# x in 4 KB runs with its norm weights, first tiles split by engine, squares on GpSimd, a new tile order

## The chip, the cores and the metric

The kernel runs on one core of one Trainium2 chip. The metric is the device time of one execution in microseconds; less is better. Inside the core, five engines run programs of their own and meet at semaphores: PE (TensorE, matrix products), ACT (ScalarE), DVE (VectorE), POOL (GpSimd) and SP, which here only issues the transfers.

## The reference, cut to what matters

One decoder layer over 512 tokens and 1024 channels. The part that the change touches is the beginning: the norm of x and the wide projection of it.

```python
u = rms_norm(h, g_pre)            # h = x, [512, 1024]
cols = u @ w_in                   # 1024 -> 6272 columns
# A: block-sparse attention on q, k, v, gate columns (512 each)
# B: RWKV-7 recurrence on r, k, v, gate (512 each) and two low-rank inputs (64 + 64)
merged = sigmoid(gate_a) * (yA @ p_a) + sigmoid(gate_b) * (yB @ p_b)
h = h + rms_norm(merged @ w_out, g_post)
h = h + sigmoid(h @ w_ple_gate) * (p @ w_ple_up)
```

## The kernel before, in words

Everything lies transposed: 128 channels on the partitions, 512 tokens along the row, eight channel groups kt = 0 to 7. A product in full precision is done as three products of a cheaper kind: every operand is split into a high part (the value rounded to the matmul's format) and a low part (the rest), and `mm3` runs high by high, high by low and low by high. ACT makes the high parts by a copy, DVE the low parts by a subtraction.

w_in is cut into tiles of 128 columns, named by what they give: k, r, v, z (RWKV), Q, K, V, Z (attention), g (merge gates), four or sixteen of each. A tile takes 24 matmuls of 512 columns (8 channel groups by 3 products). Four tiles come first (`first_tiles`, line 649): k0, r0, v0 and the low-rank tile, and these multiply x itself, high and low (`xh`, `xl`, made by `x_split`, line 615, times the norm weight g_pre), since the norm's factor for each token can be applied to their results. Their weights are split in quarters by `first_split`. The tiles k0 and r0 are run in two halves of 256 tokens (their results are called `s` in the rows), so that they can begin when half of x is there; then v0 (`y`) and the low-rank tile (`c`). Ahead of them stand `WARM` = 12 matmuls on zeros that keep TensorE busy while the first data comes.

In the meantime `squares` and `pre_norm` (lines 707 and 714) square x, add the eight channel groups (three additions on DVE, over 1024, 512 and 256 elements of a row), sum over the partitions by a product with ones (`g<-ones,rms`), take the inverse root in a string of short DVE instructions, spread it by a product with the identity (`g<-cst,rb`), and make the normed u: eight products `uf` on DVE, eight copies `u_hi` on ACT, eight subtractions `u_lo` on DVE.

From there the other 44 tiles (`FILL`, line 44; `fill`, line 819; results `pp`) run on u. They are the filling: whenever the recurrence or the attention has no product ready, PE takes the next matmul of a fill tile. After them come the merge, the output projection and the last gate, in the order `LAST`.

The order on each engine is fixed when the program is built: the kernel is written as streams (generators), and `Plan` picks again and again the stream that can start first by assumed durations, with ranks (`RC`, `RR_`, `RI` and others) and bonuses between streams that are close. An engine then runs its list strictly in order. `Queue` (line 310) assumes when a transfer has landed. All transfers are issued by SP, in program order: half of x in two pieces, the vectors (`vec`, g_pre among them), the first weights.

Of the kernel before, what the change touches and what calls it, by code (L numbers as in the profile page):

```python
# [26 lines left out]
F32 = mybir.dt.float32  # L27
# [8 lines left out]
T = 512  # L36
# [7 lines left out]
FILL = """  # L44
K0 g0 r1 Z0 v1 V0 g1 Q0 g2 k1 r2 g3 k2 z0 Q1 Z1 v2 K1 V1 z1 r3 k3 g4
v3 g5 V2 Z2 g6 K2 g7 g8 Q2 g9 g10 g11 V3 Z3 K3 Q3 z2 g12 g13 z3 g14 g15
"""
# [5 lines left out]
GROUPS = (0, 1), (2,), (3,)  # L53
WARM = 12
LARGE = 0.01796
BW = 0
SAME = 0.03
URGENT = 5
RC, RR_, RI, RP, RA, RE, RW = 10, 7, 6, 4, 5, 4, 3
WR, WA, WC = 0.0, 0.0, 0.0  # L60

VEC = {}
_o = 0
for _n, _k in (("g_pre", 8), ("g_post", 8), ("mu", 17), ("a0", 4), ("k_k", 4), ("k_a", 4), ("r_k", 4),
               ("ln_w", 4), ("ln_b", 4), ("w0", 4)):
    VEC[_n] = _o
    _o += _k
# [243 lines left out]
class Queue:  # L311


    def __init__(self, real, plan):
        self.real, self.plan = real, plan
        self.issue = self.move = 0.0

    def dma_start(self, out, src):
        self.real.dma_start(out, src)
        spot = lambda a: (a.tensor.name, a.offset)  # L320
        self.issue = max(self.issue, self.plan.cur.now, self.plan.written.get(spot(src), ("Q", 0.0))[1]) + 0.5
        self.move = max(self.move, self.issue + 1.6) + math.prod(out.shape) / 92000
        self.plan.written[spot(out)] = "Q", self.move
        return self.move


@with_exitstack
def hybrid_kernel(ctx: ExitStack, tc, xT, pT, wu, wda, wmain, wpab, wout, wpg, vec_in, cst_in, oneh, relb, wupa,
# [208 lines left out]
    st = start_stack.enter_context(tc.tile_pool(name="start", bufs=1))  # L537
    x_sb = st.tile([128, 8, T], F32, name="x_sb")
    xh = st.tile([128, 8, T], F32R, name="xh")
# [12 lines left out]
    def load_x(h, q):  # L552
        ks = slice(4 * q, 4 * q + 4)
        plan.marks[f"dx{h}{q}"] = sp.dma_start(x_sb[:, ks, HALF[h]], xT[:, ks, HALF[h]])

    def load_first(src):
        raw, plan.marks[f"dw{len(sraw)}"] = load_raw(src, st if len(sraw) > 1 else None)
        sraw.append(raw)

    load_x(0, 0)  # L560
    there = sp.dma_start(vec, vec_in)
    load_first(wmain[0])
    load_x(0, 1)
# [51 lines left out]
    def x_split(h, kt):  # L615
        c = HALF[h]
        yield ("wait", f"dx{h}{kt // 4}")
        if kt % 2:
            yield "A"
            act.activation(xh[:, kt, c], x_sb[:, kt, c], AF.Copy, scale=V("g_pre", kt))  # L620
        else:
            yield "D"
            dve.tensor_scalar(xh[:, kt, c], x_sb[:, kt, c], V("g_pre", kt), None, op0=OP.mult)
        yield "D"
        dve.scalar_tensor_tensor(xl[:, kt, c], x_sb[:, kt, c], V("g_pre", kt), xh[:, kt, c].bitcast(F32),
                                 op0=OP.mult, op1=OP.subtract)
        plan.mark(f"x{h}{kt}")
# [79 lines left out]
    def squares(h, sq):  # L707
        for kt in range(8):
            yield ("wait", f"dx{h}{kt // 4}")
            yield "A"  # L710
            act.activation(sq[:, kt, :], x_sb[:, kt, HALF[h]], AF.Square)
            plan.mark(f"sq{h}{kt}")

    def pre_norm():
        pb, fb = yield from take()
        sqs = [st.tile([128, 8, 256], F32, tag="sq", name="sq", bufs=2) for _ in range(2)]
        for h, sq in enumerate(sqs):
            plan.spawn(squares(h, sq), 0.1)
        for h, sq in enumerate(sqs):
            for kt in range(8):  # L720
                yield ("wait", f"sq{h}{kt}")
            for w in (4, 2):
                yield "D"
                dve.tensor_tensor(sq[:, 0:w], sq[:, 0:w], sq[:, w:2 * w], op=OP.add)
            yield "D"
            dve.tensor_tensor(rms[:, HALF[h]], sq[:, 0], sq[:, 1], op=OP.add)
        yield "P"
        for tt in range(4):
            pe.matmul(pb[:, tt:tt + 1], rms[:, tt * 128:tt * 128 + 128], ones, start=True, stop=True)
        ms, rs, tn = (st.tile([128, 4], F32, name=n) for n in ("ms4", "rs4", "tn4"))  # L730
        yield "D"
        dve.tensor_scalar(ms, pb[:, 0:4], 1.0 / 1024, RMS_EPS, op0=OP.mult, op1=OP.add)
        plan.mark(fb)
        yield from rsqrt(rs, ms, tn)
        rb = at.tile([128, T], F32, tag="bt0", name="rb4").rearrange("p (a b) -> p a b", b=128)
        yield "D"
        dve.tensor_scalar(rb, rs.unsqueeze(2).to_broadcast([128, 4, 128]), RS, None, op0=OP.mult)
        pr, fr = yield from take()
        yield "P"
        for tt in range(4):  # L740
            pe.matmul(pr[:, tt * 128:tt * 128 + 128], rb[:, tt, :], ident, start=True, stop=True)
        for kt in range(8):
            yield "D"
            tag = ("kb", "rb", "rb", "vb", "vb", "zt", "zt", "est")[kt]
            uf = (at if kt > 4 else krv).tile([128, T], F32, tag=tag, name="uf", bufs=BUFS[tag])
            dve.scalar_tensor_tensor(uf, x_sb[:, kt, :], V("g_pre", kt), pr, op0=OP.mult, op1=OP.mult)
            plan.spawn(norm_split(kt, uf), 0.5)
        yield "A"
        act.activation(rms, pr, AF.Copy)
        plan.mark(fr)  # L750
        plan.mark("rms")

    def norm_split(kt, uf):
        yield "A"
        act.activation(u_hi[:, kt, :], uf, AF.Copy)
        yield "D"
        dve.tensor_tensor(u_lo[:, kt, :], uf, u_hi[:, kt, :].bitcast(F32), op=OP.subtract)
        plan.mark(f"u{kt}")
# [60 lines left out]
    def fill(kinds):  # L819
        for i, (w, j) in enumerate(kinds):  # L820
            if w in "krv" and j >= BUFS[w + "b"]:
                yield ("wait", f"used{w}{j - BUFS[w + 'b']}")
            if w == "z":
# [187 lines left out]
    def rwkv(j):  # L1011
# [88 lines left out]
        dve.tensor_tensor(k2, k, fk, op=OP.mult)  # L1100
        plan.mark(f"usedk{j}")
        yield "D"
# [41 lines left out]
        yield ("wait", f"sv{j}")  # L1144
        plan.mark(f"usedv{j}")

        for g in range(4):
            if g:
                yield ("wait", f"gram{j}.{g - 1}")
            if g == 2:  # L1150
                yield ("wait", f"w1{j}.4")
                plan.mark(f"usedr{j}")
            gA, fA = yield from take()
# [282 lines left out]
    def late_tiles():  # L1436
# [25 lines left out]
        for q in range(2):  # L1462
            yield ("wait", f"o{2 + q}")
            sp.dma_start(F["x"][:, 4 * q:4 * q + 4, :], xT[:, 4 * q:4 * q + 4, :])

# [147 lines left out]
def arrange(inputs):  # L1613
# [7 lines left out]
    a = {  # L1621
        "xT": tiles(g["x"][0].T),
        "pT": tiles(g["p"][0, 0].T),
# [29 lines left out]
```

## Time and profile before

| | |
|---|---|
| median of 3 runs | 575.1 us (573.61 to 575.67) |
| the profiled execution | 574.87 us, of which 573.1 us are the span |
| PE busy | 558.6 us (97%) |
| DVE busy | 419.7 us (73%) |
| ACT busy | 298.7 us (52%) |
| POOL busy | 3.9 us (1%) |
| mean DMA rate | 116 GB/s |
| mean granted TensorE clock | 0.994 of full |

The span is what the profiler saw from the first to the last instruction; the time is 1.77 us longer. The share of busy time is an average over a short beginning, in which PE waits, and a long rest, in which it hardly does.

### The profile page before, as it was taken

To read this page: it belongs to the slowest core of one execution; us is meant where nothing else is said; L and a number is where in the kernel's file an instruction comes from. 1 tells how busy PE (TensorE), PEld (TensorE's weight loads), DVE (VectorE), ACT (ScalarE), POOL (GpSimd) and SP (SyncE) were. 2 spreads that over 40 slices of the span, in tenths; PEclk is the share of its full clock that TensorE was granted. 3 is DMA by queue.
4 is the path that set the end of the run, shared out by engine and by line. 5 is a ranking of instruction groups with operands and counts; after the bars stand their busy time and mean duration, and the time that the engine had idled before them with its cause. 6 is when DMAs were issued, how large, how long until landed. Compare 5 with 4: busy or idle time off the path is not lost.

```text
span 573.1 us, 10476 instructions
## 1 busy us (share of the span) xinstructions
PE 558.6 (97%) x4080; PEld 454.0 (79%) x4080; DVE 419.7 (73%) x973; ACT 298.7 (52%) x610; POOL 3.9 (1%) x17
## 2 busy tenths in 40 slices
PE   5899999999999999999999999999999999999997
PEld 3886878777777787777777877788788898999886
DVE  5997678879878887789986775659756666478623
ACT  6638563665357576546664565566433245543311
POOL 0000100000000000000000000000000000000000
PEclk8899999999999999999999999999999999999999
DMA  8321523124321112422322213325356458502211
GB/s 297 134 73 65 207 98 112 55 75 143 108 79 68 56 62 66 159 94 74 111 93 87 82 56 111 125 79 187 125 202 219 168 188 325 202 10 66 93 38 55
DMA packets 27417, 66.61 MB, mean 116 GB/s; under 512 B 2879, under 2 KB 7487, under 8 KB 27112
## 3 DMA queue, kind: packets, MB, share of 16 engines
q1 hardware_dynamic: 27368, 65.95, 33.0%
q8 instruction: 32, 0.52, 0.4%
q14 instruction: 17, 0.14, 0.1%
HBM read 56.74 MB, written 11.82 MB: 120 GB/s over the span
## 4 chain that ended last, share of the span: by engine, by line
PE 88%; DVE 7%; DMA 2%; ACT 1%; issue 1%; SPq 0%; DVEq 0%; ACTq 0%
PE pp L295 50%; PE s L295 13%; PE g L295 12%; PE c L295 8%; PE y L295 5%; DMA x_sb<-xT 1%; DVE Ep L295 1%; DVE wlo L295 1%; DVE xl L295 1%; DMA yf<-yB_dram 1%; DVE X L295 0%; DVE h_lo L295 0%; ACT En L295 0%; DVE Y L295 0%; DVE xh L295 0%
## 5 line engine op out<-in xcount | busy, mean ns | idle before, releaser
L295 PE MATMUL pp<-u_hi,whi 128*128 128x512 f32 x360 | 145.7, 405 | 0.4 <-DVE kl L295 0.4
L295 PE MATMUL pp<-u_lo,whi 128*128 128x512 f32 x360 | 145.3, 403 | 0.0
L295 PE MATMUL pp<-u_hi,wlo 128*128 128x512 f32 x360 | 144.6, 402 | 0.0
L295 ACT ACTIVATE whi<-raw 128x1024 fp32r<-128x1024 f32 (+1 forms) x86 | 71.5, 847 | 78.8 <-PE pp L295 51.2
L295 DVE TENSOR_TENSOR wlo<-raw,whi 128x1024 fp32r<-128x1024 f32 (+1 forms) x86 | 81.6, 960 | 32.7 <-ACT whi L295 32.2
L295 PEld LDWEIGHTS pp<-u_hi,whi 128*128 128x128 f32 x360 | 67.7, 188 | 14.8 <-PE pp L295 0.8
L295 PEld LDWEIGHTS pp<-u_hi,wlo 128*128 128x128 f32 x360 | 67.7, 188 | 13.2 <-issue 0.7
L295 PEld LDWEIGHTS pp<-u_lo,whi 128*128 128x128 f32 x360 | 67.8, 188 | 12.2 <-issue 0.6
L295 ACT ACTIVATE P<-P,sml 128x128 f32<-128x128 f32 (+3 forms) x32 | 17.8, 557 | 15.8 <-DVE sml L295 14.6
L295 DVE SCALAR_TENSOR_TENSOR SV<-c,D,sd 64x64 f32<-64x64 f32 x56 | 15.9, 283 | 5.9 <-PE c L295 4.8
L295 ACT ACTIVATE sd<-SV,D 64x64 f32<-64x64 f32 x56 | 19.3, 344 | 1.0
L295 DVE TENSOR_TENSOR W<-g,cst 64x128 f32<-64x128 f32 (+1 forms) x64 | 17.2, 290 | 0.7
L295 DVE CUSTOM_DVE_ANT_0 P<-s,bt 128x128 f32<-128x128 f32 (+3 forms) x32 | 14.7, 485 | 3.9 <-PE s L295 3.8
L295 PEld LDWEIGHTS c<-SV,W 128*64 128x64 f32 x240 | 9.5, 136 | 9.5 <-issue 5.9
L295 PE MATMUL pp<-m_hi,whi 128*128 128x512 f32 (+1 forms) x48 | 17.0, 354 | 0.0
L295 PE MATMUL pp<-m_lo,whi 128*128 128x512 f32 (+1 forms) x48 | 17.0, 354 | 0.0
L295 PE MATMUL pp<-m_hi,wlo 128*128 128x512 f32 (+1 forms) x48 | 17.0, 354 | 0.0
L295 ACT ACTIVATE Xt<-y 128x512 f16<-128x512 f32 x20 | 11.9, 594 | 9.7 <-PE y L295 9.6
L295 DVE TENSOR_TENSOR Z<-c,lvl 128x512 f16<-128x512 f32 x20 | 13.7, 687 | 3.3 <-PE c L295 3.2
L295 ACT ACTIVATE W<-g 128x128 f32<-128x128 f32 x32 | 7.1, 274 | 15.8 <-PE g L295 15.8
L295 PE MATMUL g<-W,BK 64*128 64x128 f32 x128 | 15.0, 310 | 0.0
L295 DVE SCALAR_TENSOR_TENSOR t<-gb,pp 128x512 f32<-128x512 f32 (+1 forms) x8 | 5.2, 655 | 12.5 <-PE pp L295 12.5
(362 smaller groups left out, 1251.1 us busy)
## 6 DMA issues: line engine op xcount, KB each, us to landing
raw<-wmain SPq DMA_DIRECT2D x48, 512.0 KB, 3.3
g_dram<-gst SPq DMA_DIRECT2D x16, 256.0 KB, 2.0
raw<-wpab SPq DMA_DIRECT2D x8, 512.0 KB, 3.3
raw<-wout SPq DMA_DIRECT2D x8, 512.0 KB, 3.4
raw<-wpg SPq DMA_DIRECT2D x8, 512.0 KB, 4.1
bb_dram<-b_dram SPq DMA_DIRECT2D x4, 640.0 KB, 7.1
x_sb<-xT SPq DMA_DIRECT2D x4, 512.0 KB, 9.3
bt<-bb_dram SPq DMA_DIRECT2D x8, 256.0 KB, 3.3
```

The source lines that it names most:

```text
L295: r = f(out, *args, **kw)
```

## The change

What it does, part by part:

- x lies in device memory as runs of 4 KB for each partition (two halves of tokens, each in two groups of four channel groups; before, runs of 1 KB), with the eight columns of g_pre ahead of the first run; `vec` loses g_pre and is loaded after x.
- `x_split`: ACT makes all 16 high parts of x (8 before), DVE all 16 low parts (as before) and none of the high ones (8 before).
- `squares`: for the first half of the tokens, POOL squares (two instructions of 1024) and adds (1024, 512, 256); for the second half, ACT squares in two instructions of 1024 (eight of 256 before) and DVE adds.
- `norm_split`: some of the `u_lo` go to POOL, where the plan finds it free.
- `FILL` in a new order, 11 warming matmuls for 12, ranks `RR_` 9 for 7 and `RI` 2 for 6, other assumed transfer times; the mark by which a fill tile of k, r or v waits for its buffer has a name of its own (`done...`), which the end of a product no longer sets.
- x is read a second time, late, in four transfers instead of two.

```diff
@@ -42,8 +42,8 @@
 FILL = """
-K0 g0 r1 Z0 v1 V0 g1 Q0 g2 k1 r2 g3 k2 z0 Q1 Z1 v2 K1 V1 z1 r3 k3 g4
-v3 g5 V2 Z2 g6 K2 g7 g8 Q2 g9 g10 g11 V3 Z3 K3 Q3 z2 g12 g13 z3 g14 g15
+r1 Z0 v1 K0 V0 Q0 g0 k1 g1 r2 g2 k2 Q1 g3 z0 Z1 v2 K1 V1 z1 r3 g4 v3
+g5 k3 V2 Z2 g6 K2 g7 g8 Q2 g9 g10 g11 V3 Z3 K3 Q3 z2 g12 z3 g13 g14 g15
 """
...
@@ -51,17 +51,18 @@
 GROUPS = (0, 1), (2,), (3,)
-WARM = 12
+WARM = 11
 LARGE = 0.01796
-BW = 0
+BW = 0.0
+SQ = 0.1
 SAME = 0.03
 URGENT = 5
-RC, RR_, RI, RP, RA, RE, RW = 10, 7, 6, 4, 5, 4, 3
+RC, RR_, RI, RP, RA, RE, RW = 10, 9, 2, 4, 5, 4, 3
 WR, WA, WC = 0.0, 0.0, 0.0
...
 _o = 0
-for _n, _k in (("g_pre", 8), ("g_post", 8), ("mu", 17), ("a0", 4), ("k_k", 4), ("k_a", 4), ("r_k", 4),
+for _n, _k in (("g_post", 8), ("mu", 17), ("a0", 4), ("k_k", 4), ("k_a", 4), ("r_k", 4),
                ("ln_w", 4), ("ln_b", 4), ("w0", 4)):
...
@@ -313,15 +314,15 @@
         self.real, self.plan = real, plan
-        self.issue = self.move = 0.0
+        self.issue, self.move = 0.74, 0.0
...
         self.issue = max(self.issue, self.plan.cur.now, self.plan.written.get(spot(src), ("Q", 0.0))[1]) + 0.5
-        self.move = max(self.move, self.issue + 1.6) + math.prod(out.shape) / 92000
-        self.plan.written[spot(out)] = "Q", self.move
-        return self.move
+        self.move = max(self.move, self.issue + 0.8) + math.prod(out.shape) / 92000
+        self.plan.written[spot(out)] = "Q", self.move + 0.9
+        return self.move + 0.9
...
@@ -535,7 +536,8 @@
     st = start_stack.enter_context(tc.tile_pool(name="start", bufs=1))
-    x_sb = st.tile([128, 8, T], F32, name="x_sb")
+    xg = st.tile([128, 8 + 8 * T], F32, name="xg")
+    g_pre, x_sb = xg[:, 0:8], xg[:, 8:].rearrange("p (h k t) -> p h k t", h=2, k=8)
     xh = st.tile([128, 8, T], F32R, name="xh")
...
@@ -550,20 +552,21 @@
     def load_x(h, q):
-        ks = slice(4 * q, 4 * q + 4)
-        plan.marks[f"dx{h}{q}"] = sp.dma_start(x_sb[:, ks, HALF[h]], xT[:, ks, HALF[h]])
+        o = 8 + 1024 * (2 * h + q)
+        c = slice(o if h or q else 0, o + 1024)
+        plan.marks[f"dx{h}{q}"] = sp.dma_start(xg[:, c], xT[:, c])
...
     load_x(0, 0)
-    there = sp.dma_start(vec, vec_in)
     load_first(wmain[0])
...
     load_x(1, 1)
+    there = sp.dma_start(vec, vec_in)
     load_first(wmain[8])
...
@@ -615,14 +618,11 @@
         yield ("wait", f"dx{h}{kt // 4}")
-        if kt % 2:
-            yield "A"
-            act.activation(xh[:, kt, c], x_sb[:, kt, c], AF.Copy, scale=V("g_pre", kt))
-        else:
-            yield "D"
-            dve.tensor_scalar(xh[:, kt, c], x_sb[:, kt, c], V("g_pre", kt), None, op0=OP.mult)
-        yield "D"
-        dve.scalar_tensor_tensor(xl[:, kt, c], x_sb[:, kt, c], V("g_pre", kt), xh[:, kt, c].bitcast(F32),
+        g = g_pre[:, kt:kt + 1]
+        yield "A"
+        act.activation(xh[:, kt, c], x_sb[:, h, kt], AF.Copy, scale=g)
+        yield "D"
+        dve.scalar_tensor_tensor(xl[:, kt, c], x_sb[:, h, kt], g, xh[:, kt, c].bitcast(F32),
                                  op0=OP.mult, op1=OP.subtract)
...
@@ -705,25 +705,31 @@
     def squares(h, sq):
-        for kt in range(8):
-            yield ("wait", f"dx{h}{kt // 4}")
-            yield "A"
-            act.activation(sq[:, kt, :], x_sb[:, kt, HALF[h]], AF.Square)
-            plan.mark(f"sq{h}{kt}")
+
+        for q in range(2):
+            ks = slice(4 * q, 4 * q + 4)
+            yield ("wait", f"dx{h}{q}")
+            if h:
+                yield "A"
+                act.activation(sq[:, ks], x_sb[:, h, ks], AF.Square)
+            else:
+                yield "G"
+                pool.tensor_tensor(sq[:, ks], x_sb[:, h, ks], x_sb[:, h, ks], op=OP.mult)
+        e = dve if h else pool
+        for w in (4, 2):
+            yield e.key
+            e.tensor_tensor(sq[:, 0:w], sq[:, 0:w], sq[:, w:2 * w], op=OP.add)
+        yield e.key
+        e.tensor_tensor(rms[:, HALF[h]], sq[:, 0], sq[:, 1], op=OP.add)
+        plan.mark(f"sum{h}")
...
         for h, sq in enumerate(sqs):
-            plan.spawn(squares(h, sq), 0.1)
-        for h, sq in enumerate(sqs):
-            for kt in range(8):
-                yield ("wait", f"sq{h}{kt}")
-            for w in (4, 2):
-                yield "D"
-                dve.tensor_tensor(sq[:, 0:w], sq[:, 0:w], sq[:, w:2 * w], op=OP.add)
-            yield "D"
-            dve.tensor_tensor(rms[:, HALF[h]], sq[:, 0], sq[:, 1], op=OP.add)
+            plan.spawn(squares(h, sq), SQ)
+        for h in range(2):
+            yield ("wait", f"sum{h}")
         yield "P"
...
@@ -743,7 +749,9 @@
             uf = (at if kt > 4 else krv).tile([128, T], F32, tag=tag, name="uf", bufs=BUFS[tag])
-            dve.scalar_tensor_tensor(uf, x_sb[:, kt, :], V("g_pre", kt), pr, op0=OP.mult, op1=OP.mult)
+            halves = lambda a: a.rearrange("p (h t) -> p h t", h=2)
+            dve.scalar_tensor_tensor(halves(uf), x_sb[:, :, kt], g_pre[:, kt:kt + 1], halves(pr), op0=OP.mult,
+                                     op1=OP.mult)
             plan.spawn(norm_split(kt, uf), 0.5)
...
@@ -753,8 +761,9 @@
         act.activation(u_hi[:, kt, :], uf, AF.Copy)
-        yield "D"
-        dve.tensor_tensor(u_lo[:, kt, :], uf, u_hi[:, kt, :].bitcast(F32), op=OP.subtract)
+        e = pool if plan.t["G"] + 0.7 < plan.t["D"] else dve
+        yield e.key
+        e.tensor_tensor(u_lo[:, kt, :], uf, u_hi[:, kt, :].bitcast(F32), op=OP.subtract)
         plan.mark(f"u{kt}")
...
@@ -819,7 +828,7 @@
             if w in "krv" and j >= BUFS[w + "b"]:
-                yield ("wait", f"used{w}{j - BUFS[w + 'b']}")
+                yield ("wait", f"done{w}{j - BUFS[w + 'b']}")
             if w == "z":
...
@@ -1098,7 +1107,7 @@
         dve.tensor_tensor(k2, k, fk, op=OP.mult)
-        plan.mark(f"usedk{j}")
+        plan.mark(f"donek{j}")
         yield "D"
```

The table of numbers sets the order on each engine, so here is what stands there at the places of which the prediction speaks. ACT from its first work on data, before (`xh` high part of x, `sq` squares, `whi`, `qs`, `shi` high parts of the four first weight tiles):

```order
L295 ACTIVATE xh<-x_sb,vec 128x256 x2
L295 ACTIVATE sq<-x_sb 128x256 x2
L295 ACTIVATE whi<-raw 128x256 x4
L295 ACTIVATE xh<-x_sb,vec 128x256 x2
L295 ACTIVATE sq<-x_sb 128x256 x2
L295 ACTIVATE whi<-raw 128x256 x4
L295 ACTIVATE xh<-x_sb,vec 128x256 x2
L295 ACTIVATE sq<-x_sb 128x256 x2
L295 ACTIVATE xh<-x_sb,vec 128x256 x2
L295 ACTIVATE sq<-x_sb 128x256 x2
L295 ACTIVATE qs<-raw 128x256 x4
L295 ACTIVATE shi<-raw 128x256 x4
```

The same place after the change:

```order
L296 ACTIVATE xh<-xg 128x256 x4
L296 ACTIVATE whi<-raw 128x256 x4
L296 ACTIVATE xh<-xg 128x256 x4
L296 ACTIVATE whi<-raw 128x256 x4
L296 ACTIVATE xh<-xg 128x256 x8
L296 ACTIVATE qs<-raw 128x256 x4
L296 ACTIVATE shi<-raw 128x256 x4
L296 ACTIVATE sq<-xg 128x1024 x2
```

All squares that stay on ACT now stand behind the first weights; before, pairs of them stood between the pieces of x and the weights, and eight more behind `shi`.

DVE at its start, before (`xl` low part of x, `wlo`, `kh`, `slo` low parts of the weights):

```order
L295 SCALAR_TENSOR_TENSOR xl<-x_sb,vec,xh 128x256 x2
L295 TENSOR_TENSOR wlo<-raw,whi 128x256
L295 TENSOR_SCALAR xh<-x_sb,vec 128x256
L295 SCALAR_TENSOR_TENSOR xl<-x_sb,vec,xh 128x256 x2
L295 TENSOR_SCALAR xh<-x_sb,vec 128x256
L295 SCALAR_TENSOR_TENSOR xl<-x_sb,vec,xh 128x256 x2
L295 TENSOR_TENSOR wlo<-raw,whi 128x256 x3
```

DVE from its first instruction after the change:

```order
L296 SCALAR_TENSOR_TENSOR xl<-xg,xh 128x256 x4
L296 TENSOR_TENSOR wlo<-raw,whi 128x256 x4
L296 SCALAR_TENSOR_TENSOR xl<-xg,xh 128x256 x4
L296 TENSOR_TENSOR wlo<-raw,whi 128x256 x4
L296 SCALAR_TENSOR_TENSOR xl<-xg,xh 128x256 x8
L296 TENSOR_TENSOR kh<-raw,qs 128x256 x4
```

Before, one quarter of the first tile's weights stood ahead of the second group of x, and the other three behind it; after, all four quarters stand ahead of it, and the second tile's ahead of the second half of the tokens.

POOL behind its first fills, after the change (before, the row behind `mix_89` was the fill of `reset`, far later):

```order
L296 MEMSET mix_89 128x1
L296 ISA
L296 TENSOR_TENSOR sq<-xg 128x1024 x2
L296 TENSOR_TENSOR sq<-sq 128x1024
L296 TENSOR_TENSOR sq<-sq 128x512
L296 TENSOR_TENSOR rms<-sq 128x256
L296 TENSOR_TENSOR u_lo<-uf,u_hi 128x512 x4
```

Five arithmetic instructions of the norm and four of the eight `u_lo` stand on POOL now. On PE the number of matmuls is the same but for one warming matmul; runs of fill matmuls are broken by other products 146 times before and 141 times after, and the order from the merge to the end is the same.

## Rows read from the trace of the kernel before

**Rows 1.** Page, busy time: share of the span by engine.

```profile
PE 558.6 (97%) x4080; PEld 454.0 (79%) x4080; DVE 419.7 (73%) x973; ACT 298.7 (52%) x610; POOL 3.9 (1%) x17
```

**Rows 2.** Windows: stretch and length, then each engine's busy time, PEclk, DMA share, GB/s.

```profile
10.00:15.00 5.00, 2.64 (x14) 2.44 (x13) 4.86 (x14) 4.94 (x15) 0.00 (x0) 0.55 1.06 390
35.00:40.00 5.00, 5.00 (x23) 4.06 (x22) 4.92 (x8) 2.54 (x4) 0.00 (x0) 1.00 0.00 0
```

**Rows 3.** Windows, the long middle, columns as in rows 2.

```profile
100.00:412.00 312.00, 310.35 (x2707) 244.18 (x2705) 247.94 (x613) 182.63 (x381) 0.00 (x0) 1.00 0.28 95
```

**Rows 4.** Timeline, PE, 0 to 20 us: start, length, instruction, idle before.

```profile
8.83 0.38 PE L295 MATMUL s<-xh,whi 128*128 128x256 f32 x1 [2.21 <-ACT whi L295]
...
12.62 0.58 PE L295 MATMUL s<-xh,wlo 128*128 128x256 f32 x1 [2.36 <-DVE wlo L295]
...
14.28 0.41 PE L295 MATMUL s<-xh,whi 128*128 128x256 f32 x1
...
14.49 0.41 PE L295 MATMUL s<-xl,whi 128*128 128x256 f32 x1
...
18.34 0.39 PE L295 MATMUL s<-xh,wlo 128*128 128x256 f32 x1 [1.52 <-DVE wlo L295]
```

**Rows 5.** Chain that ended last, in order of time: start, length, piece.

```profile
18.34 8.52 PE s L295 x70
...
31.25 0.89 PE g L295 x8
...
34.23 5.59 PE c L295 x24
39.82 4.08 PE pp L295 x18
```

**Rows 6.** Timeline, ACT, 0 to 20 us.

```profile
4.92 0.91 ACT L295 ACTIVATE xh<-x_sb,vec 128x256 fp32r<-128x256 f32 x2 [2.68 <-DMA vec<-vec]
...
8.36 1.34 ACT L295 ACTIVATE whi<-raw 128x256 fp32r<-128x256 f32 x4 [1.92 <-DMA raw<-wmain]
```

**Rows 7.** Timeline, DVE, 0 to 20 us.

```profile
9.78 0.35 DVE L295 TENSOR_SCALAR xh<-x_sb,vec 128x256 fp32r<-128x256 f32 x1 [0.54 <-DMA x_sb<-xT]
...
10.17 0.88 DVE L295 SCALAR_TENSOR_TENSOR xl<-x_sb,vec,xh 128x256 fp32r<-128x256 f32 x2
...
17.87 1.42 DVE L295 TENSOR_TENSOR wlo<-raw,whi 128x256 fp32r<-128x256 f32 x4
```

**Rows 8.** Transfers, stretch 5 to 8 us: packets moved, rate, sizes.

```profile
DMA packets 635, 1.00 MB, mean 332 GB/s; under 512 B 31, under 2 KB 512, under 8 KB 635
```

**Rows 9.** Transfers, stretch 13 to 16 us.

```profile
DMA packets 542, 1.17 MB, mean 391 GB/s; under 512 B 55, under 2 KB 230, under 8 KB 542
```

**Rows 10.** Timeline, DVE, 20 to 48 us.

```profile
21.90 1.94 DVE L295 TENSOR_TENSOR sq<-sq 128x1024 f32<-128x1024 f32 x2
...
23.87 0.42 DVE L295 TENSOR_TENSOR rms<-sq 128x256 f32<-128x256 f32 x1
...
27.69 0.16 DVE L295 TENSOR_SCALAR ms<-g 128x4 f32<-128x4 f32 x1
...
30.02 1.22 DVE L295 TENSOR_TENSOR wlo<-raw,whi 128x1024 fp32r<-128x1024 f32 x1
...
32.17 1.41 DVE L295 SCALAR_TENSOR_TENSOR uf<-x_sb,vec,g 128x512 f32<-128x512 f32 x2 [0.50 <-PE g L295]
```

**Rows 11.** Timeline, DVE, 33 to 48 us.

```profile
41.75 1.35 DVE L295 TENSOR_TENSOR u_lo<-uf,u_hi 128x512 fp32r<-128x512 f32 x2
```

**Rows 12.** Timeline, POOL and DVE side by side, 50 to 62 us.

```profile
57.77 2.25 POOL L295 MEMSET W<- 64x512 f32 x4
...
57.87 0.69 DVE L295 TENSOR_TENSOR ad_x<-wa,ad_x 64x512 fp32r<-64x512 f32 x1 [1.35 <-ACT ad_x L295]
```

**Rows 13.** Timeline, PE, around 100 us: a fill run behind a break.

```profile
100.00 0.50 PE L295 MATMUL pp<-u_hi,wlo 128*128 128x512 f32 x1
100.34 0.40 PE L295 MATMUL pp<-u_hi,whi 128*128 128x512 f32 x1
```

More of the change, by code (lines that the diff above doesn't have):

```diff
@@ L1144, in rwkv @@
         yield ("wait", f"sv{j}")
-        plan.mark(f"usedv{j}")
+        plan.mark(f"donev{j}")
         for g in range(4):
@@ L1151, in rwkv @@
                 yield ("wait", f"w1{j}.4")
-                plan.mark(f"usedr{j}")
+                plan.mark(f"doner{j}")
             gA, fA = yield from take()
@@ L1463, in late_tiles @@
             yield ("wait", f"o{2 + q}")
-            sp.dma_start(F["x"][:, 4 * q:4 * q + 4, :], xT[:, 4 * q:4 * q + 4, :])
+            for h in range(2):
+                o = 8 + 1024 * (2 * h + q)
+                sp.dma_start(F["x"][:, 4 * q:4 * q + 4, HALF[h]],
+                             xT[:, o:o + 1024].rearrange("p (k t) -> p k t", k=4))
     def load_wu(n):
@@ L1621, in arrange @@
     a = {
-        "xT": tiles(g["x"][0].T),
+        "xT": np.concatenate([cols(g["g_pre"][0]), tiles(g["x"][0].T).reshape(128, 8, 2, 256).transpose(0, 2, 1, 3)
+                              .reshape(128, -1)], 1),
         "pT": tiles(g["p"][0, 0].T),
@@ L1629, in arrange @@
         "wpg": chunks(g["w_ple_gate"][0]),
-        "vec": np.concatenate([cols(g[n][0]) for n in ("g_pre", "g_post", "mu_shift", "a0", "k_k", "k_a", "r_k",
+        "vec": np.concatenate([cols(g[n][0]) for n in ("g_post", "mu_shift", "a0", "k_k", "k_a", "r_k",
                                                        "ln_x_w", "ln_x_b", "w0")], 1),
```

## Prediction

> **What bounds the kernel now.** I read the page's busy shares first: PE works 97% of the span [rows 1], so a change can only take PE work away, or PE's waiting, or what PE loses at a lower clock. Then the windows, to see where PE waits. In the middle, from 100 to 412 us, it is busy 310.35 of 312 us [rows 3]: there, 1.65 us are all that a better order could win in waits. In the beginning it is another kernel: between 10 and 15 us PE is busy 2.64 of 5 us, its granted clock is 0.55, DVE and ACT are busy 4.86 and 4.94, and the transfers move 390 GB/s [rows 2]. The timeline names the stops: 2.21 us until ACT's first high part of the weights, then 2.36 and 1.52 us until a low part from DVE [rows 4], 6.1 us together. Between the last two, a matmul of 256 columns starts every 0.21 us (14.28, 14.49) [rows 4]; from 18.34 on, 70 of them take 8.4 us, 0.12 each [rows 5]. The clock had gone to half after the first two stops, and some 18 matmuls (96 less the 70 and about 8 at first) paid 0.095 us more, 1.7 us.
>
> The chain in order of time then gives PE's course: k0 and r0 from 18.34, the low-rank tile from 34.23 in 5.59 us, the first fill matmul at 39.82 [rows 5]. From 39.82 on PE only has to work off a list whose sum is fixed. So the question of this change is at what time the fill begins, and whether what comes behind stays as dense. One more thing to see: between 35 and 40 us DVE is busy 4.92 of 5 us [rows 2], with the products `uf` and `u_lo` (0.70 and 0.68 us each) [rows 10, 11]. DVE is nearly the bound of the whole beginning; a fill that begins earlier needs u earlier, that is, less DVE work ahead of it.
>
> **The change, part by part.**
>
> *DVE work ahead of the fill.* It loses 8 `xh` at 0.35 [rows 7], 2.8 us; the additions of one half, 1.94 + 0.42 = 2.4 us [rows 10]; four `u_lo` at 0.68 [rows 11], 2.7 us. That is 7.9 us. ACT gains 8 `xh` at about 0.45 (0.91 for two) [rows 6], 3.6 us, and loses eight squares of 256, which go to POOL, 2.6 us at the price of `whi` (1.34 for four) [rows 6]; its other eight become two of 1024, at most 1.34 each by the same row. ACT idles later, so the 1 us more is hidden if the squares stand behind the weights, as they do now.
>
> *Arrival.* The first `xh` waits till 4.92 for `vec` [rows 6], which stood behind x; now the weights come with x. Where most packets are 1 KB the queue moves 332 GB/s, where large ones prevail 391 [rows 8, 9]: 0.52 MB of x take 1.3 instead of 1.6 us. The first weights land at 8.36 [rows 6], with x's first piece and `vec` ahead of them, the second piece of x at 9.78 [rows 7]. By the rates alone they would have come about 2 us sooner, so some lag of the slowest engine is in these times, and I don't know if it stays. Bounds for the first weights: 8.36 less 0.3 and the 0.15 of `vec`, 7.9, if the lag stays; 5.9 if it goes. I take 7.0, and for the second piece, between 9.1 and 6.9, 8.0.
>
> *The walk through the first tiles.* x at 4.0: ACT four `xh` until 5.8, `whi` 7.0 to 8.35, four `xh` to 10.0, the second tile's `whi` to 11.35, eight `xh` to 14.7, `qs` and `shi` to 17.3, squares to 19.4. DVE follows by 0.2 us: `xl` cost 0.40 to 0.44, `wlo` 0.35 [rows 7], less than what ACT needs, so it waits for ACT. PE begins at 7.5, is fed with little gap until 10.4, then has r0's first half to 13.3, and, as the last `xl` comes at 14.9, runs on to the end of both tiles at 18.9 (96 matmuls by 0.12 are 11.5 us). Before, this end is 18.34 + 8.4 = 26.7. Then nine matmuls of v0 (0.23 each by 5.59 for 24) [rows 5] to 21.0. The sum of squares is ready at 19.4 + 2.4 = 21.9, DVE's additions of the second half ending last; PE waits 0.9. The product with ones takes 0.9 [rows 5], to 22.8; the root string, which takes 2.3 us from 27.69 to 30.02, and a `wlo` of 1.22 ahead of it [rows 10], lie beside the other 15 matmuls of v0 (to 26.3). The second short product ends at 27.2, the low-rank tile at 32.8, where the fill begins. u's last part: eight `uf` and four `u_lo` from 27.3 are 8.3 us, 35.6; the fill needs it after 21 matmuls, at 37.7. So 39.82 − 32.8 = 7.0 us, against 7.9 us of DVE work removed: two ways to about the same number.
>
> *POOL's price.* No row shows POOL in arithmetic. Its nearest rows are fills: 2.25 us for four of 512 [rows 12], 1.1 us for 1024 elements. One write stream at this rate is the lower bound, two reads and a write one after the other, 3.3 us, the upper; I take 2.2. The five instructions of the half (1024 x 3 + 512 + 256) are then 8.4 us (4.2 to 12.7): from 4.0, with the second piece at 8.0, done at about 14.3, 7 us ahead of 21.9. That cover is the slack for anything that POOL does at its first arithmetic instruction (the order shows an `ISA` row ahead of it). Four `u_lo` are 4.5 us beside DVE's eight `uf`, hidden too.
>
> *What POOL does to DVE.* DVE's `xl`, `wlo` and `u_lo` read two operands from SBUF, and so do POOL's instructions. The only row of both at work has POOL filling: `ad_x` took 0.69 beside it [rows 12], as much as a `u_lo` with no POOL work beside it (0.68) [rows 11]. So one end is no cost; the other is that DVE stands still for all of POOL's 8.4 us, less the 1 us in which it would wait anyway, 7.4. The row is nearest to nothing, but a fill reads nothing; I take a quarter of the way, 2.0 us on DVE's path to the first tiles. The Trainium skill (SBUF — State Buffer, section "Who interferes with whom") says that a DVE instruction with two SBUF inputs contends with a GpSimd instruction that reads SBUF, that the first to issue keeps the shared ports for its whole length, and that one which only writes does not contend. The filling row agrees with its last clause and tests none of the others; by the rule the cost would be the far end, and the sum that of the first rival.
>
> *The new order of the middle.* PE's matmuls are the same but one warming one, which only shortens a wait. 146 runs of fill become 141; a first fill matmul behind a break starts its successor 0.34 us later instead of 0.23 [rows 13, 5], so 5 x 0.11 = 0.55 us. The new ranks, the new tile order and the plan's other times I count at nothing: 1.65 us of waits cannot shrink by much [rows 3], and they could double. The second read of x moves the same bytes late, where the order of all engines is unchanged: nothing.
>
> **Sum**, against the profiled execution, 574.87 (span 573.1 and 1.77 around it): 574.87 − (7.0 − 2.0) − 0.55 = 569.3. The execution lies 0.2 below the median of 575.1, so it may stand for it.
>
> **Rivals.**
>
> *POOL holds DVE up whole.* 7.4 us later in the first tiles eat the 7.0: 574.87 − 7.0 + 7.4 − 0.55 = 574.7, no change. For it: all of DVE's work at that time has two SBUF operands, and DVE paces PE. Against: the first POOL square falls when DVE waits for ACT and the weights. It decides from about 5 us of delay.
>
> *The clock, slower than before.* PE begins at 7.5 after an idle 1.3 us, and is fed in drips until 10.4. Before, it was granted half the clock after stops of 2.21 and 2.36 us [rows 4]. If it falls at once and only returns when both tiles are through, 96 matmuls pay 0.095, 9.1 us, and v0's 24 pay 0.23, 5.5 us; 2.0 of the stops go with that: 574.87 − 5.0 − 0.55 + 12.6 = 581.9. Against: the stops are shorter, and each group of three matmuls (0.35 us) meets a pace of 0.41 to 0.45. It makes the kernel slower when over 58 matmuls of 256 columns (5.55 / 0.095) run at half clock.
>
> *The middle gives back.* The new ranks put the inverse behind attention; if its waits come to 4 us instead of 1.65 and another break or two, 572.3. Against: the counts of fill matmuls left behind the last attention tile are alike in the two orders (38 and 37).
>
> **How the numbers follow.** The forecast 0.55, with its own range 566.5 to 571.7 (no delay of DVE, early weights; or 4 us of delay); POOL whole 0.2 (573 to 576); the middle 0.15 (571 to 574); the clock 0.1 (over 577). Half a per cent, 2.9 us, is about what a measurement of this kernel can tell from no change: faster is below 572.2. That is 0.55, most of 0.15 halved, and a little of POOL whole: 0.66 faster, 0.25 same, 0.09 slower. The range leaves out the clock and the lucky end: 566 to 575.5.
>
> **What would show it.** `xh` beginning near 4.0; the first matmul of x near 7.5; the two tiles through near 19 to 21, the fill begun at 33 to 35; clock 1.0 throughout. POOL's squares at 2.2 us for 1024, and `xl`, `wlo` at 0.40 and 0.35 beside them: if their starts are spaced by POOL's lengths, the first rival holds. The sum of squares by DVE, not POOL, releasing the product with ones. After the fill's beginning, PE busy but for 2 to 3 us. Wrong would be the prediction if the weights landed at 8 again and the clock fell, or if POOL's half came last.

## The result and the profile after

The changed kernel takes 579.57 us (median of 4 runs, 579.09 to 580.15) where the kernel before takes 575.1: a ratio of 1.0082 with an interval of 1.0061 to 1.0104, so it is slower, by about 4.5 us. The forecast was 569.3 with a range of 566.0 to 575.5: the sign was wrong, and the time lies outside the range. The profiled execution took 579.34 us, 577.6 of them span, at a mean granted clock of 0.990. Of the runs in the table below, one is left out of its ratio: an execution of "only the squares write" that took 772.85 us at a granted clock of 0.656.

The page's row of busy times, answering to [rows 1]: POOL has gone from 3.9 to 17.7 us, and PE works 1.5 us more although it has one matmul less.

```profile
PE 560.1 (97%) x4079; PEld 454.5 (79%) x4079; DVE 423.2 (73%) x964; ACT 296.1 (51%) x598; POOL 17.7 (3%) x26
```

First, when does the fill begin? The chain in order of time (start, length, what), answering to [rows 5]:

```profile
0.74 4.40 DMA xg<-xT
12.63 2.70 DVE wlo L296 x3
15.78 11.87 PE s L296 x83
...
35.05 5.59 PE c L296 x24
40.63 3.43 PE pp L296 x15
```

In the chain the low-rank tile begins at 35.05 (34.23 before) and takes the same 5.59 us. Counted in PE's timeline, the first fill matmul starts at 40.47, where it started at 39.66 before; the forecast was 32.8, or 34.8 with the 2.0 us allowed for POOL. The start has gained nothing; it lost 0.8 us. PE's timeline at the beginning shows one long stop where [rows 4] had three:

```profile
7.23 0.39 PE L296 MATMUL s<-xh,whi 128*128 128x256 f32 x1 [1.11 <-ACT whi L296]
...
12.76 0.58 PE L296 MATMUL s<-xh,wlo 128*128 128x256 f32 x1 [4.93 <-DVE wlo L296]
13.14 0.41 PE L296 MATMUL s<-xh,whi 128*128 128x256 f32 x1
```

PE begins near 7.5, as forecast, runs two matmuls, and waits 4.93 us for the first low part of the weights. The windows (columns as in [rows 2]) give the clock behind that stop, and two later stretches:

```profile
10.00:15.00 5.00, 2.24 (x10) 2.18 (x11) 5.00 (x5) 5.00 (x15) 4.55 (x3) 0.50 0.98 377
15.00:20.00 5.00, 4.83 (x24) 4.54 (x24) 5.00 (x14) 3.46 (x8) 0.00 (x0) 0.54 0.41 131
...
65.00:70.00 5.00, 2.25 (x11) 1.51 (x9) 4.35 (x15) 3.42 (x6) 0.00 (x0) 1.00 0.01 2
...
100.00:412.00 312.00, 310.01 (x2658) 242.69 (x2656) 247.05 (x608) 178.03 (x369) 0.00 (x0) 1.00 0.29 97
```

From 10 to 20 us the clock is granted at half (0.50, 0.54: the 1.2 GHz level), as it was for a shorter while before (0.55 and 0.77 in these windows). The long middle is as dense as before [rows 3]: 1.99 us without PE work instead of 1.65. But between 65 and 70 PE is idle for 2.75 of 5 us, and no such hole was there before:

```profile
65.00:70.00 5.00, 5.00 (x24) 4.16 (x24) 4.64 (x14) 0.92 (x2) 0.00 (x0) 1.00 0.28 112
```

What holds the first low part? DVE's timeline and, behind it, POOL's:

```profile
5.71 4.50 DVE L296 SCALAR_TENSOR_TENSOR xl<-xg,xh 128x256 fp32r<-128x256 f32 x4 [5.71 <-ACT xh L296]
10.13 5.20 DVE L296 TENSOR_TENSOR wlo<-raw,whi 128x256 fp32r<-128x256 f32 x4
15.25 1.66 DVE L296 SCALAR_TENSOR_TENSOR xl<-xg,xh 128x256 fp32r<-128x256 f32 x4
16.84 1.42 DVE L296 TENSOR_TENSOR wlo<-raw,whi 128x256 fp32r<-128x256 f32 x4
```

```profile
5.21 1.89 POOL L296 TENSOR_TENSOR sq<-xg 128x1024 f32<-128x1024 f32 x1 [3.84 <-DMA xg<-xT]
7.73 2.20 POOL L296 TENSOR_TENSOR sq<-xg 128x1024 f32<-128x1024 f32 x1 [0.62 <-DMA xg<-xT]
10.01 3.83 POOL L296 TENSOR_TENSOR sq<-sq 128x1024 f32<-128x1024 f32 x2
13.92 0.80 POOL L296 TENSOR_TENSOR rms<-sq 128x256 f32<-128x256 f32 x1
```

POOL's five instructions run from 5.21 to 14.72. The eight DVE instructions beside them take 9.70 us; the next eight, the same two forms with POOL silent, take 3.08. ACT, working beside both all the time, is not slowed: its four `xh` take 1.71 us, its four `whi` 1.32. The view of the tile `wlo` from 9 to 16 us gives the spread of the four:

```profile
L296 DVE TENSOR_TENSOR wlo<-raw,whi x4: 412/1222/2570, 10.1 to 14.9; 128x256 fp32r<-128x256 f32 x4
```

One took the 412 ns that it takes alone, one 2570 ns. Narrow windows of the two timelines show single instructions, here the first two `wlo` and POOL's two additions beside them:

```profile
10.13 2.57 DVE L296 TENSOR_TENSOR wlo<-raw,whi 128x256 fp32r<-128x256 f32 x1
...
12.63 1.50 DVE L296 TENSOR_TENSOR wlo<-raw,whi 128x256 fp32r<-128x256 f32 x1
```

```profile
10.01 2.41 POOL L296 TENSOR_TENSOR sq<-sq 128x1024 f32<-128x1024 f32 x1
...
12.50 1.34 POOL L296 TENSOR_TENSOR sq<-sq 128x512 f32<-128x512 f32 x1
```

The `wlo` end at 12.70 and 14.12, each 0.28 us behind the end of POOL's addition (12.42 and 13.84). So do three others of the eight; the remaining three start while POOL has no instruction running and take their own length. An instruction of DVE thus stands until POOL's is through; it doesn't run at a lower rate.

Then, how long from the start of the fill to the start of the merge? Both kernels, windows cut at those two points (the first of before, the second of after):

```profile
39.66:420.79 381.13, 378.88 (x3046) 297.92 (x3045) 299.12 (x722) 220.77 (x446) 3.04 (x9) 1.00 0.29 100
```

```profile
40.47:425.33 384.86, 379.69 (x3045) 297.31 (x3044) 302.59 (x727) 218.70 (x439) 5.59 (x11) 1.00 0.30 99
```

This stretch, with the same matmuls, has become 3.7 us longer: 2.9 us more without PE work (5.17 against 2.25) and 0.8 us more of it. From the merge to the end nothing changed. So the 4.5 us of span are 0.8 in the start and 3.7 in the middle. Most of the middle is one wait, in PE's timeline at 68.96, and DVE's timeline tells what it hangs on:

```profile
65.82 0.39 PE L296 MATMUL pp<-u_lo,whi 128*128 128x512 f32 x1
68.96 0.50 PE L296 MATMUL pp<-u_hi,wlo 128*128 128x512 f32 x1 [2.75 <-DVE wlo L296]
```

```profile
63.26 0.75 DVE L296 SCALAR_TENSOR_TENSOR vb<-pp,omu,mix 128x512 f32<-128x512 f32 x1 [3.06 <-ACT mix L296]
...
64.53 1.76 DVE L296 COPY Z<-id 128x1024 f16<-128x1024 f16 x5
...
67.02 0.68 DVE L296 TENSOR_TENSOR kl<-pp,kh 64x512 fp32r<-64x512 f32 x1 [0.45 <-ACT kh L296]
...
67.70 1.21 DVE L296 TENSOR_TENSOR wlo<-raw,whi 128x1024 fp32r<-128x1024 f32 x1
```

The low part of the weights of V0, the fifth fill tile now, stands on DVE behind `kl`, the low part of K0's result. That waits for ACT's `kh` (65.79), and that for PE's last product of K0. So PE, through with K0, can do only the two products of V0 that need no low part, and then waits for a chain that begins with its own last product of K0: `kh`, `kl`, `wlo`. From 65.79 to the end of `wlo` at 68.91 that chain is 3.1 us long.

### The profile page after: what moved, and what is told of

Read it like the earlier page. It is cut to its first block, busy times and chain, and to the rows that moved or that the text cites. A ratio compares the mean times of both kernels' runs of the same rounds, so it can differ in the third digit from the quotient of the medians.

```text
span 577.6 us, 10488 instructions
## 1 busy us (share of the span) xinstructions
PE 560.1 (97%) x4079; PEld 454.5 (79%) x4079; DVE 423.2 (73%) x964; ACT 296.1 (51%) x598; POOL 17.7 (3%) x26
## 4 chain that ended last, share of the span: by engine, by line
PE 89%; DVE 6%; ACT 3%; issue 1%; DMA 1%; DVEq 0%
PE pp L296 50%; PE s L296 14%; PE g L296 12%; PE c L296 8%; PE y L296 5%; DVE wlo L296 1%; DVE Ep L296 1%; DMA xg<-xT 1%; ACT En L296 1%; DMA bvl<-bv_dram 0%; DVE xl L296 0%; DVE h_lo L296 0%; DVE kl L296 0%; DVE Y L296 0%; ACT kka L296 0%
## 5 line engine op out<-in xcount | busy, mean ns | idle before, releaser
L296 DVE TENSOR_TENSOR wlo<-raw,whi 128x1024 fp32r<-128x1024 f32 (+1 forms) x86 | 85.2, 1003 | 27.0 <-ACT whi L296 26.4
L296 PEld LDWEIGHTS pp<-u_lo,whi 128*128 128x128 f32 x360 | 67.7, 188 | 14.3 <-issue 1.8
L296 ACT ACTIVATE P<-P,sml 128x128 f32<-128x128 f32 (+3 forms) x32 | 17.7, 555 | 16.0 <-DVE sml L296 15.9
L296 PE MATMUL s<-xh,wlo 128*128 128x256 f32 x32 | 10.6, 331 | 4.9 <-DVE wlo L296 4.9
```

The lines of the kernel that those rows point to most:

```text
L296: r = f(out, *args, **kw)
```

## The experiments

Two questions: is it POOL's reading that eats the start, and is it the order of the middle that costs the rest, or the start that spoils it? All times are medians; ratios are to the kernel before, run beside them on the same chip (where its median was 575.1, 575.02 or 575.82). "Fill" is the start of the first fill matmul, "middle" the stretch from there to the first product of the merge. Both are read from the profiled execution, whose clock can differ from that of the median: with the old start and the new middle it took 577.67 us.

| kernel | time, us | ratio, 95% | fill | middle | of it without PE work |
|---|---|---|---|---|---|
| before | 575.1 | 1 | 39.66 | 381.13 | 2.25 |
| after | 579.57 | 1.0082 [1.0061, 1.0104] | 40.47 | 384.86 | 5.17 |
| POOL only writes | 572.8 | 0.9965 [0.9950, 0.9980] | 33.60 | 385.81 | 4.77 |
| only the squares write | 572.0 | 0.9938 [0.9919, 0.9956] | 32.38 | 385.67 | 4.90 |
| no POOL, planned anew | 580.96 | 1.0110 [1.0078, 1.0142] | 32.43 | 394.42 | 11.18 |
| layout alone | 574.43 | 0.9982 [0.9964, 0.9999] | 39.40 | 380.84 | 1.90 |
| old tile order in after | 588.26 | 1.0243 [1.0211, 1.0274] | 40.18 | 393.73 | 9.09 |
| new start, old middle | 572.76 | 0.9953 [0.9931, 0.9975] | 32.46 | 386.61 | 5.01 |
| old start, new middle | 579.36 | 1.0075 [1.0052, 1.0098] | 38.03 | 385.57 | 4.53 |
| one `wlo` moved | 581.1 | 1.0097 [1.0079, 1.0115] | 40.56 | 387.3 | 5.73 |

**POOL only writes.** In place of each of POOL's nine arithmetic instructions stand a copy of one column, which keeps its waits, and two fills of its whole output with a constant. Everything else stands in the same order.

```diff
+        if self.key == "G" and name == "tensor_tensor":
+            f = self.write_only
...
+        self.real.tensor_copy(one(out), one(a))
...
+        for _ in range(2):
+            self.real.memset(out.bitcast(F32) if out.dtype == F32R else out, value)
```

> The changed kernel with POOL's nine arithmetic instructions replaced by fills of the same tiles (each a copy of one element, which waits for the same data, and two fills), in the same order on every other engine. The squares of the first half become constants and four low parts of u zero. Theory 1 (POOL's reads of SBUF hold up DVE's instructions with two SBUF operands): four low parts of x take 1.7 us instead of 4.5, four low parts of weights 1.4 instead of 5.2, the clock stays or falls later, the fill begins at 33 to 36 us instead of 40.6, and the time is 571 to 575. Rival (the start is slow because data and high parts come late, whatever POOL does): the fill begins past 39 and the time is 578 or more.

Measured: 572.8 us, the fill from 33.60, 6.9 us before after's. DVE's timeline, and POOL's beside it:

```profile
5.71 1.68 DVE L305 SCALAR_TENSOR_TENSOR xl<-xg,xh 128x256 fp32r<-128x256 f32 x4 [5.71 <-ACT xh L305]
7.31 1.43 DVE L305 TENSOR_TENSOR wlo<-raw,whi 128x256 fp32r<-128x256 f32 x4
```

```profile
5.44 1.96 POOL L297 MEMSET sq<- 128x1024 f32 x2
...
8.16 1.96 POOL L297 MEMSET sq<- 128x1024 f32 x2
```

POOL is as busy as before beside the same DVE instructions, and these now take 3.11 us instead of 9.70. It is POOL's reading that holds them, not its work as such.

Further on, the same trace shows two more holds. First POOL's lines, then DVE's:

```profile
13.79 3.78 POOL L294 COPY sq<-sq 128x1 f32<-128x1 f32 x1
17.63 1.11 POOL L297 MEMSET sq<- 128x512 f32 x2
```

```profile
16.08 1.43 DVE L305 TENSOR_TENSOR slo<-raw,shi 128x256 fp32r<-128x256 f32 x4
...
17.58 0.60 DVE L305 TENSOR_SCALAR hka<-vec 128x4 f32<-128x4 f32 x1
```

A copy of one column takes POOL 0.18 us at 5.20; this one takes 3.78 and ends at 17.57, right behind the last of a string of DVE's two-operand instructions (17.51). So DVE holds up POOL's reading too. And POOL's fills are not harmless to every DVE instruction: `hka`, over four elements of a row and with one operand, takes 0.60 us and ends within 0.05 us of the end of a fill, as do the three like it behind it (0.47 to 0.55); in the changed kernel, with POOL silent, it takes 0.16.

**Only the squares write.** The same edit for the first five POOL instructions alone; the four `u_lo` on POOL read again.

```diff
-        if self.key == "G" and name == "tensor_tensor":
+        if self.key == "G" and name == "tensor_tensor" and self.count("squares"):
```

> The changed kernel, same order on the other engines, with only the five instructions of the squares on POOL replaced by fills (the squares of the first half become constants); the four low parts of u on POOL read as changed. Theory: the squares alone hold up the first tiles, so the fill begins at 33.4 to 34 us as with all nine replaced, two low parts of u on DVE still take 2.4 us beside POOL's, and the time is 572.5 to 574. Rival (the low parts of u bear a part): the fill begins or goes on later by over 1 us, 574.5 or more.

Measured: 572.0 us, fill from 32.38, and a middle of 385.67, like the 385.81 where all of POOL's instructions only write:

```profile
32.38 0.39 PE L311 MATMUL pp<-u_hi,whi 128*128 128x512 f32 x1
```

So the five squares instructions are the whole of the hold that reaches PE. The hold of `u_lo` is there too, and lies off PE's path. In after, beside two POOL `u_lo` from 36.57 and two from 41.69, DVE's timeline reads:

```profile
35.09 2.72 DVE L296 SCALAR_TENSOR_TENSOR uf<-xg,g 128x512 f32<-128x512 f32 x4 [0.37 <-PE g L296]
37.85 2.45 DVE L296 TENSOR_TENSOR u_lo<-uf,u_hi 128x512 fp32r<-128x512 f32 x2
```

Two `u_lo` take 2.45 us where they took 1.35 [rows 11], and POOL's two 2.57; the four `uf`, which take one operand from SBUF and one from PSUM, take 0.68 each, as alone [rows 10], though POOL works beside the last two.

**No POOL, planned anew.** The same sums are computed without POOL: ACT squares both halves, DVE adds and makes all `u_lo`, and the planner picks the order.

```diff
-            if h:
-                yield "A"
-                act.activation(sq[:, ks], x_sb[:, h, ks], AF.Square)
-            else:
-                yield "G"
-                pool.tensor_tensor(sq[:, ks], x_sb[:, h, ks], x_sb[:, h, ks], op=OP.mult)
-        e = dve if h else pool
+            yield "A"
+            act.activation(sq[:, ks], x_sb[:, h, ks], AF.Square)
+        e = dve
...
-        e = pool if plan.t["G"] + 0.7 < plan.t["D"] else dve
+        e = dve
```

> The changed kernel with POOL's arithmetic given back: the squares of the first half on ACT in two instructions of 1024, their additions and all low parts of u on DVE. Theory 1: though DVE has 5 us more work, nothing stands still; the fill begins at 35 to 38 and the time is 572 to 576. Rival (DVE's sum of work sets the beginning, so that the work on POOL was well placed): the fill begins past 41 and the time is 580 or more.

Measured: 580.96 us. The start gains more than the theory says (fill from 32.43 for 35 to 38, PEclk 1.00 for the first 20 us), and the total misses it widely. The middle has lost 13.3 us against before and 9.6 against after. PE's waits (who waits for whom: us in total, times, longest) are many small ones, none of them in the kernel before at that size:

```profile
PE s L296 <- ACT prh L296: 1.9, 1, 1.9
PE s L296 <- DVE P L296: 1.8, 1, 1.8
PE g L296 <- DVE rnb L296: 1.5, 1, 1.5
...
PE pp L296 <- ACT u_hi L296: 1.1, 2, 0.6
PE pp L296 <- ACT vc L296: 1.0, 1, 1.0
```

PE's matmuls are the same, but 8.9 us more of the middle than in before are without PE work. The planner, with other times in the start, had picked another order for the 390 us behind it. So the order of the middle is a question of its own.

**Layout alone.** The kernel before with x in 4 KB runs and the norm weights ahead of it, nothing else.

```diff
-        plan.marks[f"dx{h}{q}"] = sp.dma_start(x_sb[:, ks, HALF[h]], xT[:, ks, HALF[h]])
+        plan.marks[f"dx{h}{q}"] = sp.dma_start(xg[:, c], xT[:, c])
```

> The kernel before with the new layout of x alone: runs of 4 KB, norm weights ahead of the first, vectors behind x, four late transfers. Theory (the layout is worth little, since the first high part now waits for the whole first piece of x): first high part at 5.0 to 5.3 instead of 4.92, second piece 0.5 to 1 us earlier, time 573.5 to 575.5. Rival (arrival bounds the beginning): 572 or less.

Measured: 574.43 us, a ratio of 0.9982 [0.9964, 0.9999]; fill from 39.40, 0.26 earlier. The layout is worth 0.6 us at the median and some 2 us at most by the interval, as the theory says. The first `xh` starts at 5.23 (4.92 before), but the first `whi` at 6.65 (8.36) and the `xh` of the second piece at 7.88 (9.78), so most of the data came sooner than it says; the clock then stood at half for longer (PEclk 0.50 and 0.53 from 10 to 20 us, 0.55 and 0.77 before), and what the arrival alone is worth isn't shown.

**Old tile order in after.** The changed kernel with the `FILL` and the ranks of before.

```diff
-RC, RR_, RI, RP, RA, RE, RW = 10, 9, 2, 4, 5, 4, 3
+RC, RR_, RI, RP, RA, RE, RW = 10, 7, 6, 4, 5, 4, 3
```

> The changed kernel with the tile order and the ranks of before, all else as changed. Theory 2 (the wait of 2.75 us of the fifth fill tile for its low parts at 69 us belongs to the new order of tiles): that wait goes and the time is 576 to 577.5. Rival (it comes from DVE being late after the beginning, whatever the order): a wait of over 2 us stays somewhere before 100 us and the time is 579 to 581.

Measured: 588.26 us, which neither side expected: a middle of 393.7. The wait for V0 is gone, and one of 2.1 us for `kl` stands near 53 us instead. The old tile order isn't good in itself; it was good with the plan in which it was found. The new one repairs 8.9 us of what the new start does to the plan, and stays 3.7 short.

**New start, old middle.** The start of the kernel without POOL, and from the norm on, the order of before, each engine's picks written out as a list in place of the planner's choice. This is a complete kernel.

```diff
+        for label, engine in PICKS:
...
+            s = [s for s in streams if not s.done and s.label == label and s.want == engine]
```

> The start of the kernel with no POOL arithmetic (new layout, ACT high, DVE low, ACT squares), and from the last product of the norm on every engine in the order of the kernel before (its tile order, ranks and buffer marks), forced by a list of picks. Theory (the order behind the start has a price of its own, 381.1 us from fill to merge in the old one, 384.9 in the changed one, 394 in the one that was planned anew): fill from 32.4 to 33.6, fill to merge 381 to 383, time 565 to 568.5. Rival (the stretch grows because an earlier fill finds DVE and ACT further behind, whatever the order): fill to merge 387 or more, time 571 or more.

Measured: 572.76 us, 0.5% below before (0.9953 [0.9931, 0.9975]): it beats both kernels, and is the fastest here that computes all of the layer. Of the 7.2 us of earlier fill, 5.5 are lost again in the middle; the result is closer to the rival's number than to the theory's. PE's waits:

```profile
PE pp L436 <- DVE kl L436: 2.0, 1, 2.0
...
PE pp L436 <- ACT u_hi L436: 0.6, 1, 0.6
PE pp L436 <- DVE u_lo L436: 0.5, 2, 0.2
```

PE now reaches the fill before u is complete (the last `u_lo` ends at 40.3, 8 us behind the first fill matmul), and then waits for `kl`, which DVE does behind that. By the windows 2.8 us more of the middle are without PE work than in before, and PE's work is 2.7 us longer; the granted clock is 0.83 between 50 and 60 us, right behind the wait for `kl`, which is 1.7 us of that.

**Old start, new middle.** The converse: the kernel before up to the norm, and behind it the order of after, from a list in the same way; all `u_lo` are on DVE. Against the changed kernel:

```diff
-            for h in range(2):
...
+            for kt in range(8):
+                yield ("wait", f"sq{h}{kt}")
...
+        for label, engine in PICKS:
```

> The start of the kernel before (old layout, old split, all squares on ACT) and from the last product of the norm on every engine in the order of the changed kernel (its tile order and ranks), forced by a list of picks. Theory: fill begins at 39.8 and fill to merge takes 384 to 386, the time is 578 to 579.5. Rival (the longer middle is a consequence of the changed start): fill to merge 381 to 382.5, time 574.5 to 576.

Measured: 579.36 us and a middle of 385.57, as the theory says; the fill starts at 38.03, 1.8 us ahead of it, in an execution whose clock stood at half for a shorter while (PEclk 0.68 and 0.98 from 10 to 20 us, against 0.55 and 0.77). PE's timeline has the same wait at the same instruction, to the hundredth:

```profile
66.50 0.79 PE L435 MATMUL pp<-u_hi,wlo 128*128 128x512 f32 x1 [2.75 <-DVE wlo L435]
```

It is 2.75 us also where POOL only writes (at 62.06) and where only the squares do (at 60.84). The new order brings this wait along whenever the fill begins; it is not the late start that makes it.

**One `wlo` moved.** The changed kernel with V0's `wlo` on DVE ahead of the six copies (`AT`, `Z`) and `kl`, nothing else moved.

DVE's rows there, against the changed kernel's:

```diff
 vb<-pp,omu,mix 128x512
+wlo<-raw,whi 128x1024
 AT<-cst 128x1024
 Z<-id 128x1024 x5
...
 kl<-pp,kh 64x512
...
-wlo<-raw,whi 128x1024
```

> The changed kernel with one DVE instruction moved: the low part of the fifth fill tile's weights (V0) stands right behind the second value tile's result, ahead of six copies of constants and of K0's low part, which waits for the end of its tile. All else in place. Theory: the wait of 2.75 us at 69 us goes and nothing takes its place, 576.3 to 577.3. Rival (the copies are late next, and the wait comes back behind them): 578.5 or more.

Measured: 581.1 us. The wait for V0 is gone, and the next one is larger:

```profile
72.19 1.09 PE L436 MATMUL g<-cst,rnb 128*128 128x128 f32 x4 [3.90 <-DVE rnb L436]
72.93 0.78 PE L436 MATMUL pp<-u_hi,wlo 128*128 128x512 f32 x1
73.51 0.63 PE L436 MATMUL pp<-u_hi,whi 128*128 128x512 f32 x1
```

The instructions that V0's `wlo` passed come 0.9 to 1.4 us later (`Z` at 65.96 for 64.53, `kl` at 67.91 for 67.02), and the string behind them that ends in `rnb` is what PE waits for now. So the wait was not that of one instruction in a wrong place, as the theory had it; it moved along a DVE that is busy 4.47 of the 5 us from 65 to 70. (The matmuls at 0.63 instead of 0.40 run at half the clock, behind the stop: PEclk 0.54 from 70 to 75 us.)

## Why the prediction was wrong

**What POOL does to DVE: the step that failed.** It was charged 2.0 us, a quarter of the way from nothing to 7.4, because the nearest row had POOL filling beside an `ad_x` that kept its 0.69 us [rows 12]. That row is right and says nothing of reading: POOL's fills cost DVE's two-operand instructions nothing here either, its reads hold them up whole. The eight DVE instructions lost 6.6 us, the fill 6.9 to 8.1 us (40.47 against 33.60 and 32.38), which is the far end, and with it the first rival (574.7) had the time of the start right. Not by its mechanism alone, though: of the 8.1 us to the kernel whose squares only write, about 5 are the stop for `wlo` (PE's third matmul of `s` starts at 12.76 instead of 7.82), and about 3 the half clock behind it (27 matmuls in the 6.6 us from 12.76, which take 3.2 at 0.12 each), a term that this rival didn't have. The Trainium skill (SBUF — State Buffer, section "Who interferes with whom") gives this rule, which the prediction quoted and weighed below a row that couldn't test it; the trace agrees: two SBUF operands against a reading POOL are held (`xl`, `wlo`, `u_lo`), one SBUF operand is not (`uf`), and POOL's fills do not hold the first kind. That fills are harmless to all of DVE would be too much said (`hka`, above).

**The walk through the first tiles held.** Without POOL's reads the fill begins at 32.38 to 33.60, against 32.8 forecast; PE begins at 7.23, against 7.5. Inside it, x came later than the 4.0 taken (the first `xh` starts at 5.17; the transfer takes 4.40 us from its issue) and the weights sooner than 7.0, which cancelled: part of the agreement is luck. POOL's price was near, 1.89 and 2.20 us for 1024 against 2.2; its sum is done at 14.7, against 14.3, and never is what the product with ones waits for.

**The new order, counted at −0.55: the second step that failed.** Fewer breaks and unchanged waits were expected; the middle costs 3.7 us more in after and 4.4 more behind the old start. In both, 2.75 us are the wait for V0; behind the old start 1.7 more are the clock after it (PEclk 0.66 from 65 to 70). The reason given was the 1.65 us of waits from 100 to 412 [rows 3], and there it held (1.99): the loss lies between 40 and 100 us, where the new tile order begins and the prediction read no waits. The rival "the middle gives back" had the kind right, a wait that the new order brings, but put it on the inverse and took 4 us of waits in all, where there are 5.2. Put together, the first rival's 574.7 and this 3.7 to 4.4 in place of −0.55 are 579.0 to 579.7, and 579.57 was measured. The two failures add up to the whole error: 5.7 us in the start (40.47 against 34.8) and 4.3 in the middle.

**The clock.** It was forecast at 1.0 throughout and stood at half from 10 to 19 us, behind the 4.93 us stop, not behind the drips that the rival named. Where only the squares write, and without POOL, it stays at 1.00 for the first 20 us with the same pace of `xl` and `wlo`; where POOL only writes, it was 0.88 and 0.89 in the first two windows (to 10 and to 15 us), behind a stop of 1.93 us ahead of the first matmul, and that accounts for the 1.2 us between 33.60 and 32.38.

**What stays open.** Why the old middle isn't worth its 381 us behind the earlier start was read from one trace (u and `kl` late on DVE, then the clock) and not tested by moving DVE's work. No run tried an order searched anew for the start without POOL; the 5.5 us between 386.6 here and 381.1 in before are a gap that no order seen here closes. Why the wait for V0 turns into a longer one for `rnb` was read from one trace as well. About 1 us of after's middle beside the wait for V0 was not traced to a place.

## What to carry to other kernels

Price an instruction that is moved to an idle engine by what it holds up on the engine that it relieves: here squares and additions of which 2.4 us came from DVE cost DVE 6.6 us. Where the only row for a disputed cost differs in the very thing that matters (a fill reads nothing), it is no reason to go near its end of the range. And an order that was searched for one set of times belongs to them: taking POOL's work back, an edit of the first 40 us, cost 9.6 us in the 390 behind them when it was planned anew (394.4 against 384.9), so keep the order and the edit apart when measuring, as the kernels with written-out picks do.

## What the runs showed of the hardware

- GpSimd's reading instructions held DVE's two-operand instructions until they were through: five of eight ended 0.28 us behind one, and a `wlo` of 0.41 us took up to 2.57. DVE's products with one SBUF operand (`uf`, 0.68 us) and ACT (1.71 for four `xh`) kept their times beside them.
- The hold goes the other way too: beside a string of DVE's two-operand instructions a GpSimd copy of one column took 3.78 us instead of 0.18. And beside a GpSimd fill of 128x512, DVE's `hka` over 128x4 took 0.60 us instead of 0.16, while `xl` and `wlo` kept their times beside fills (1.68 and 1.43 for four).
- A stop of PE does not always cost the clock behind it: behind the same wait of 2.75 us for V0 the first matmul took 0.50 us in after, with PEclk 1.00 in that window, and 0.79 behind the old start, with 0.66. The six runs of the kernel with the new start and old middle have spans of 569.3 us at a mean granted clock of 1.000 (twice) and 572.2 and 572.5 at 0.993, so some 3 us of its spread go with the clock.
- With runs of 4 KB instead of 1 KB, and the norm weights ahead of x, the second piece of x was in use at 7.88 us instead of 9.78; the fill began 0.26 us earlier, in an execution with a longer stretch at half clock. In the changed kernel the first piece took 4.40 us to land.
